# The last pair of heads turned through DRAM, and free places for the first turned tiles

## The chip, the cores and the metric

The kernel runs on one core of one Trainium2 chip. The metric is the time of one execution on the device in microseconds (us); the time before is the median of three runs. The engines are PE (matrix products), DVE (vector), ACT (scalar activations), POOL (GpSimd) and SP, whose queue issues most of the DMAs. DRAM is the chip's memory outside the cores; SBUF and PSUM are on the core, and PE writes its results to PSUM, eight banks of 128 x 512 float32.

## What is computed

One layer of a streaming encoder, in float32: four token mixers on `h = RMSNorm(x)`, gated and merged, then cross-attention, then a gated MLP. SEQ is 512, D_MODEL 1024. What matters here is mixer B, the forgetting attention, with 8 heads of 64 channels:

```python
s = jnp.einsum('bqhd,bkhd->bhqk', q_blk, k, preferred_element_type=jnp.float32) * scale
s = s + c_blk[..., None] - c_k[:, :, None, :]
mask = t_pos[None, :] <= tq_blk[:, None]
p = jax.nn.softmax(jnp.where(mask, s, -jnp.inf), axis=-1)
return jnp.einsum('bhqk,bkhd->bqhd', p.astype(v.dtype), v)
...
br = jnp.stack([ya, yf, yc, ys], axis=2)
proj = jnp.einsum('bsnc,ncd->bsnd', br, w_branch[l])
gates = jax.nn.sigmoid(h @ w_gate[l] + b_gate[l]).reshape(B, S, N_BRANCH, D)
mixed = jnp.sum(gates * proj, axis=2) @ w_out[l]
```

The mask is causal, so a query tile of 128 rows needs 128, 256, 384 or 512 keys. `yf` is the result of mixer B; its product with `w_branch` is the last of the four branches that the kernel adds up.

## The kernel before

Every float32 product is made as three products of a high and a low part (`mm3`: high by high, high by low, low by high), so a block of 128 output channels, 512 tokens and 1024 input channels takes 24 matrix products of 128 x 128 by 512. `channel_major` makes such a block. Weights come by SP in loads of 512 KB into two buffers `wr`; ACT and DVE split them into a high and a low tile (L198, L199).

The foreground is a list of such blocks, `mixer_jobs`. For the forgetting attention it has the projections of values and forget gates (`vf_jobs`), then for each of four pairs of heads two blocks for queries and keys (`kv_blocks`, L1199), with blocks of the gates and of branch A between them: `ga` yields 12 blocks in the order gate, gate, branch, and they stand 3 behind pair one's projections, 3 behind pair two's and 6 behind pair three's. Then the rest of the pairs is drained, and `last_branch_jobs` begins: gate, gate, branch and so on again, where a branch block (4 k-steps, one for each pair of heads) reads the result `y["f"]` of the pairs.

The pairs run in the background. `f_task` is a generator; at each `yield` it gives a cost and a time in which it isn't to be called again. `Background` (L47) calls the first two tasks of its queue at every tick (twice in a block), as long as it has credit, which grows by 0.7 of the foreground's estimated time and is at most 4. This sets the order of the program. A scheduler then orders each engine's instructions by that order and by its own estimate of when they are ready, and sets the waits.

A pair has four query tiles of 128 rows, one in each of the steps 0 to 3:

- `scores` (L830): 2 products for each head into an `sc` bank; DVE adds the bias and takes the row's minimum of the negated scores (L1129) into a tile `e`; ACT exponentiates (L1135); the two heads are scaled by ACT (L1142) and DVE (L1140). `e4()` has three buffers.
- The tile must then be turned so that keys lie on the partitions. Pairs 0 to 2 (`far`) do it through DRAM: `turn_ready` turns squares of 32 x 32 on DVE (`turn_squares`, L854) into another `e` tile, `put` (L859) stores that to DRAM, `get` (L866) loads it in another order into the low tile `ptl`, and `split_in_place` makes the high part on ACT (L872) and the low part on DVE (L873). The loads stand in steps 3 (query tiles 0, 1) and 5 (tiles 2, 3), the splits in steps 4 and 6, the products with the values in steps 5 and 7.
- Pair 3, the last, turns on PE: `to_keys_major` (L836) transposes each 128 x 128 piece with the identity (L247) into a `tr` bank, and ACT and DVE split it out of PSUM (L161, L162). It has six steps, with the values in steps 3 and 5. At its step 2 `share_now("mm")` takes the bank `tr0` from the gates' blocks.
- `pt_tiles` has two buffers each of `pth` and `ptl`; a pair of heads takes both for tiles 0 and 1, and both again for tiles 2 and 3. So a pair waits at step 3 (pair three: step 2) until the pair before it has made its last values (`f_steps[p - 1] < 8`).
- The two heads' results are in two `av` banks, the only ones; ACT and DVE add the high and the low part (L1153, L1154) and split the sum into `y["f"][0][:, p]` and `y["f"][1][:, p]`. These two tiles, of four places of 512 columns each, are made when the first pair ends.

The queries and keys of a pair lie in a tile with the tag `qk`, of which there are two.

Of the kernel before, what the change touches and what calls it, by code (L numbers as in the profile page):

```python
# [18 lines left out]
F32R = mybir.dt.float32r  # L19
# [6 lines left out]
P = 128  # L26
S = 512
# [56 lines left out]
def hybrid_layer(ctx: ExitStack, tc: tile.TileContext, a: dict, out: bass.AP):  # L84
# [21 lines left out]
    def share_now(*among):  # L106
        vars(turn_of).update(n=1, among=among)
# [102 lines left out]
    steps_of = []  # L210
# [110 lines left out]
    m1p = m1.__enter__()  # L321
# [211 lines left out]
    half = {}  # L533
# [74 lines left out]
    def y8(dtype=F32R):  # L608
        return m2p.tile([P, 4, S], dtype, tag="y8", name="y8", bufs=2)
# [5 lines left out]
    y = {}  # L615
# [249 lines left out]
    def get(d, n, pt, local):  # L865
        SP.dma_start(part_of(pt[1], n, local).bitcast(F32), d.rearrange("(a j) (b x) -> (j b) a x", j=32, b=4))  # L866

    def split_in_place(n, pt, local):
        hi, lo = (part_of(x, n, local) for x in pt)
        raw = lo.bitcast(F32)  # L870
        with tc.issue_after(evacuations[0]):
            A.copy(hi, raw)  # L872
        V.tensor_tensor(lo, raw, hi.bitcast(F32), ALU.subtract)  # L873
# [21 lines left out]
    def pt_tiles():  # L895
        return tuple(m1p.tile([P, 2, 4, 4, 32], F32R, tag=n, name=n, bufs=2) for n in ("pth", "ptl"))
# [160 lines left out]
    f_steps = {-1: 8}  # L1057

    def f_task(p, qk, v):
        f_steps[p] = 0  # L1060
        far = p < 3
        while f_steps[p - 1] < 4:
            yield 0.0, 0.5
        ck = []
        for j in range(2):
            t = m1p.tile([P, S], F32, tag="ck", name="ck", bufs=2)
            G.dma_start(t, crows[2 * p + j:2 * p + j + 1, :].rearrange("a s -> (a s)").partition_broadcast(P))
            ck.append(t)
        yield 0.0, 2.0 if p else 5.0
        es, pts, av, ready = {}, None, None, []  # L1070

        def turn_ready():
            while ready:
                qt, e, w = ready.pop()
                turned = e4()
                for j in range(2):
                    turn_squares(turned[:, j, :w], e[:, j, :w])
                es[qt] = put(turned, w)
        for step in range(8 if far else 6):
            if step in ((5, 7) if far else (3, 5)):  # L1080
                if av is None:
                    av = [bank("av"), bank("av")]
                with tc.issue_after(steps_of[0]) if far else ExitStack():
                    for j in range(2):
                        hl = v[0][:, :, 2 * p + j]
                        values(av[j], lambda kt: ((hl[:, kt], 0), (hl[:, kt], 1)), pts[j],
                               step // 2 - (2 if far else 1))
            while step == (3 if far else 2) and f_steps[p - 1] < 8:
                yield 0.0, 0.5
            f_steps[p] = step + 1  # L1090
            cost = 0.0
            if step == 4:
                turn_ready()
            if far:
                for qt in SPLITS.get(step, ()):
                    for j in range(2):
                        split_in_place(qt + 1, pts[j], qt % 2)
                    cost += 0.1 + 0.3 * qt
                for qt in GETS.get(step, ()):
                    if qt % 2 == 0:  # L1100
                        pts = [pt_tiles() for _ in range(2)]
                    d = es.pop(qt)
                    for j in range(2):
                        get(d[:, j], qt + 1, pts[j], qt % 2)
            else:
                if step == 2:
                    share_now("mm")
                for qt in {2: (0, 1), 3: (2,), 4: (3,)}.get(step, ()):
                    if qt % 2 == 0:
                        pts = [pt_tiles() for _ in range(2)]  # L1110
                    e = es.pop(qt)
                    for j in range(2):
                        to_keys_major(e[:, j], qt + 1, pts[j], qt % 2)
                    cost += 0.4 + 0.3 * qt
            if step < 4:
                qt, w = step, (step + 1) * P
                e = es[qt] = e4()
                st = m1p.tile([P, 8], F32, tag="st8", name="st8", bufs=4)
                for j in range(2):
                    head = 2 * p + j  # L1120
                    bias = m1p.tile([P, S], F32, tag="fbias", name="fbias", bufs=2)

                    G.tensor_scalar(bias[:, :w], ck[j][:, :w], -1.0, cq[:, qt, head:head + 1],  # L1123
                                    ALU.mult, ALU.add)
                    G.affine_select(out=bias[:, w - P:w], in_=bias[:, w - P:w], pattern=[[-1, P]],
                                    compare_op=ALU.is_ge, fill=BIG, base=0, channel_multiplier=1)
                    ps = bank("sc")
                    scores(ps, qk, j, qt * P, w)
                    low = V.tensor_tensor_reduce(e[:, j, :w], ps[:, :w], bias[:, :w], scale=-HD ** -0.5,  # L1129
                                                 scalar=3.0e38, op0=ALU.add, op1=ALU.min,  # L1130
                                                 accum_out=st[:, j:j + 1])
                with tc.issue_after(low.ins):
                    turn_ready()
                for j in range(2):
                    A.activation(e[:, j, :w], e[:, j, :w], AF.Exp, bias=st[:, j:j + 1],  # L1135
                                 scale=-1.0, accum_out=st[:, 4 + j:5 + j])
                V.reciprocal(st[:, 6:8], st[:, 4:6])
                for j in range(2):
                    if j:
                        V.tensor_scalar(e[:, j, :w], e[:, j, :w], st[:, 6 + j:7 + j], None, ALU.mult)  # L1140
                    else:
                        A.activation(e[:, j, :w], e[:, j, :w], AF.Copy, scale=st[:, 6 + j:7 + j])  # L1142
                cost += 0.6 + 0.0038 * w
                if far:
                    ready.append((qt, e, w))
                    cost += 0.003 * w
            yield cost, 6.5 if far and step == 5 else 4.5
        if "f" not in y:
            y["f"] = (y8(), y8())

        e = e4()
        for j in range(2):
            A.copy(e[0:HD, j], av[j][HD:P])  # L1153
            V.tensor_tensor(e[j * HD:(j + 1) * HD, 0], av[j][0:HD], e[0:HD, j], ALU.add)  # L1154
        split(e[:, 0], y["f"][0][:, p], y["f"][1][:, p])
        yield 1.8, 0.0
# [45 lines left out]
    def mixer_jobs():  # L1202
# [32 lines left out]
        ga = gate_blocks(0, "a")  # L1235
        for p in range(1, 4):
            yield from kv_blocks(p)
            for _ in range((3, 3, 6)[p - 1]):
                yield next(ga)
        yield then(lambda: bg.drain("f"))  # L1240

# [656 lines left out]
```

## Time and profile before

| | us |
|---|---|
| median of 3 runs | 1048.19 |
| lowest, highest | 1047.79, 1048.29 |
| the profiled execution | 1047.26 |
| its span on the core | 1045.5 |

The profile is one execution, seen by the hardware profiler. It gives each engine's busy time and the groups of its instructions, the chain of work that ended last (followed back from the last instruction, at each step to what released it), and timelines. The start of the span is 0. PE's instructions overlap: a product of 512 columns is in the timeline with 0.39 us, and the next starts 0.23 us after it. L247 is the line of the transposition, L241 that of every product; the tiles' names (`ps_tr`, `ps_mm`, `ps_av`, `ps_sc` for the banks, `y8b` for branch A's and `y` for the forgetting attention's results) tell them apart. In the columns of a timeline stand the start, the duration, the engine, the line, what is written and read, and in brackets the idle time before and what ended it.

### The profile page before, as it was taken

What the parts mean: (1) busy time and instruction counts of PE and PEld (TensorE: products, weight loads), DVE (VectorE), ACT (ScalarE), POOL (GpSimd) and SP (SyncE); (2) the same over time, 40 slices, a digit from 0 to 9 for tenths busy, and PEclk for the clock granted to TensorE, in tenths of its full rate; (3) what the DMA queues carried; (4) which work ended last, traced back from release to release, by engine and by line L of the source; (5) the groups of instructions that cost most, each with busy time, mean ns of one, the idle gap of its engine ahead of it and who ended that gap; (6) DMA issues with size and microseconds to landing.
All of it is one profiled execution on the core that took longest, in us unless ns stands there. A gap on an engine that the chain in (4) does not pass through costs nothing.

```text
span 1045.5 us, 14417 instructions
## 1 busy us (share of the span) xinstructions
PE 1035.8 (99%) x5235; PEld 880.7 (84%) x5235; DVE 809.6 (77%) x1241; ACT 510.6 (49%) x838; POOL 143.3 (14%) x239
## 2 busy tenths in 40 slices
PE   9999999999999999999999999999999999999997
PEld 8888888888888988888888899998888888888886
DVE  7999998677787367878577898777767777667786
ACT  5322222376565365666444566555343333445662
POOL 4001000100010123342101031121112111111001
PEclk9999999999999999999999999999999999999999
DMA  8954333334433246666338744135676676626662
GB/s 271 311 156 100 101 101 101 91 91 121 142 104 109 62 122 178 184 165 158 120 124 287 237 134 127 62 108 184 193 240 229 214 227 217 220 82 183 216 214 82
DMA packets 187453, 166.48 MB, mean 159 GB/s; under 512 B 20415, under 2 KB 159148, under 8 KB 187381
## 3 DMA queue, kind: packets, MB, share of 16 engines
q1 hardware_dynamic: 178339, 133.80, 43.1%
q10 hardware_dynamic: 6482, 23.21, 6.1%
q0 software_dynamic: 2560, 8.54, 2.7%
q8 instruction: 41, 0.67, 0.3%
q14 instruction: 31, 0.25, 0.1%
HBM read 140.74 MB, written 24.79 MB: 158 GB/s over the span
## 4 chain that ended last, share of the span: by engine, by line
PE 99%; DMA 0%; DVE 0%; issue 0%; POOL 0%; POOLq 0%; DVEq 0%; SPq 0%; ACT 0%; ACTq 0%
PE ps_mm L241 47%; PE ps_av L241 30%; PE ps_tr L241 11%; PE ps_sc L241 7%; PE ps_tr L247 2%; PE ps_mm L459 1%; PE ps_av L459 1%; DMA xs<-in_x 0%; PE ps_tr L443 0%; DVE o L1788 0%; PE ps_av L443 0%; DVE nt L438 0%; DVE ge L1183 0%; DVE nt L412 0%; POOL st_m L285 0%
## 5 line engine op out<-in xcount | busy, mean ns | idle before, releaser
L198 ACT CAST wh<-wr 128x1024 fp32r<-128x1024 f32 (+1 forms) x140 | 146.5, 1047 | 233.5 <-PE ps_mm L241 121.2
L199 DVE TENSOR_TENSOR wl<-wr,wh 128x1024 fp32r<-128x1024 f32 (+1 forms) x140 | 174.8, 1249 | 86.2 <-ACT wh L198 85.4
L241 PE MATMUL ps_mm<-hth,wh 128*128 128x512 f32 (+1 forms) x536 | 198.9, 378 | 0.0
L241 PE MATMUL ps_mm<-htl,wh 128*128 128x512 f32 (+1 forms) x536 | 198.3, 377 | 0.0
L241 PE MATMUL ps_mm<-hth,wl 128*128 128x512 f32 (+1 forms) x536 | 198.3, 377 | 0.0
L241 PE MATMUL ps_av<-hth,wh 128*128 128x512 f32 (+1 forms) x328 | 122.5, 374 | 0.0
L241 PE MATMUL ps_av<-htl,wh 128*128 128x512 f32 (+1 forms) x328 | 122.5, 373 | 0.0
L241 PE MATMUL ps_av<-hth,wl 128*128 128x512 f32 (+1 forms) x328 | 122.3, 373 | 0.0
L241 PEld LDWEIGHTS ps_mm<-hth,wl 128*128 128x128 f32 x536 | 99.0, 188 | 18.3
L241 PEld LDWEIGHTS ps_mm<-hth,wh 128*128 128x128 f32 x536 | 99.0, 188 | 17.9 <-ACT hth L161 0.3
L241 PEld LDWEIGHTS ps_mm<-htl,wh 128*128 128x128 f32 x536 | 98.9, 188 | 17.9
L694 DVE SCALAR_TENSOR_TENSOR y<-y,par,y 128x508 f32<-128x508 f32 (+29 forms) x120 | 82.5, 725 | 0.1
L241 PEld LDWEIGHTS ps_av<-hth,wh 128*128 128x128 f32 x328 | 61.6, 188 | 11.1 <-DVE e L1154 0.3
L241 PEld LDWEIGHTS ps_av<-htl,wh 128*128 128x128 f32 x328 | 61.6, 188 | 10.9
L241 PEld LDWEIGHTS ps_av<-hth,wl 128*128 128x128 f32 x328 | 61.6, 188 | 10.9
L1689 DVE TENSOR_TENSOR wl<-dw,wh 128x1024 fp32r<-128x1024 f32 x32 | 40.2, 1260 | 15.0 <-ACT wh L1688 14.7
L1688 ACT CAST wh<-dw 128x1024 fp32r<-128x1024 f32 x32 | 33.4, 1051 | 22.2 <-PE ps_mm L241 7.4
L1636 ACT ACTIVATE th<-c 128x512 f32<-128x512 f32 x22 | 13.9, 632 | 48.8 <-DVE c L621 48.8
L1123 POOL TENSOR_SCALAR fbias<-ck,cq 128x128 f32<-128x128 f32 (+3 forms) x32 | 23.4, 739 | 73.0 <-DVE st L1129 66.6
L621 DVE SCALAR_TENSOR_TENSOR c<-ps_mm,par,c 128x510 f32<-128x510 f32 (+1 forms) x44 | 32.7, 744 | 0.7
L241 PE MATMUL ps_tr<-hth,wh 128*128 128x512 f32 x80 | 31.8, 398 | 0.0
L241 PE MATMUL ps_tr<-htl,wh 128*128 128x512 f32 x80 | 31.6, 395 | 0.0
(503 smaller groups left out, 2227.9 us busy)
## 6 DMA issues: line engine op xcount, KB each, us to landing
wr<-in_w_up SPq DMA_DIRECT2D x44, 512.0 KB
wr<-in_w_in SPq DMA_DIRECT2D x38, 512.0 KB
wr<-in_w_gate SPq DMA_DIRECT2D x32, 512.0 KB
wp<-in_w_down ACTq DMA_DIRECT2D x22, 512.0 KB
sums<-wp ACTq DMA_DIRECT2D x22, 512.0 KB
dw<-sums SPq DMA_DIRECT2D x44, 256.0 KB
wr<-in_w_branch SPq DMA_DIRECT2D x16, 512.0 KB
wide<-in_w_out SPq DMA_DIRECT2D x12, 512.0 KB
```

What stands on the lines that cost most here:

```text
L198: last_weights[:] = [order(A.copy(hi, raw[:, :n])).ins, low.tensor_tensor(lo, raw[:, :n], hi.bitcast(F32), ALU.subtract).ins]
L199: low.tensor_tensor(lo, raw[:, :n], hi.bitcast(F32), ALU.subtract).ins]
L241: steps_of[:] = [PE.matmul(ps, lhs, rhs, start=start, stop=stop).ins]
L247: turns.append(PE.transpose(ps, x, ident[:n, :n]).ins)
L459: keep(PE.matmul(banks[c][:, :S // 2], w[p == 1][:, k, c * P:(c + 1) * P], ht[p == 2][:, i * 4 + k, :S // 2], start=(i, p, k) == (0, 0, 0) ...
L621: ins = V.scalar_tensor_tensor(dst[:, s:], src[:, :S - s], w(k), dst[:, s:], ALU.mult, ALU.add)
L694: ins = V.scalar_tensor_tensor(dst[:, s:], src[:, :S - s], pc("conv_dw", k * 4 + j), dst[:, s:], ALU.mult, ALU.add)
L1123: G.tensor_scalar(bias[:, :w], ck[j][:, :w], -1.0, cq[:, qt, head:head + 1], ALU.mult, ALU.add)
L1636: A.activation(th, c[:, 0], AF.Silu)
L1688: A.copy(hi, x)
L1689: V.tensor_tensor(lo, x, hi.bitcast(F32), ALU.subtract)
```

## The change

All four pairs go through DRAM in eight steps; `far` and pair three's way over PE are gone, with the change of the banks' share at its step 2. A pair's query tiles 0 and 1 no longer use `pth` and `ptl`: `first_tiles` puts them, for pairs 0 to 2, into places 2 and 3 of the two tiles of `y["f"]` (place 2 for the first head, 3 for the second), which only pairs two and three write in the end, and for pair three into a tile `half` with the tag `qk`. `y["f"]` is therefore made when a pair begins. The wait on the pair before is now for its step 6 at step 3 and for its step 8 at step 5. The gates' blocks stand 2, 3 and 7 behind the projections of pairs one, two and three. The planner's cost of a step of scores is the one that pairs 0 to 2 had.

```diff
     def f_task(p, qk, v):
         f_steps[p] = 0
-        far = p < 3
...
         yield 0.0, 2.0 if p else 5.0
+        if "f" not in y:
+            y["f"] = (y8(), y8())
         es, pts, av, ready = {}, None, None, []
+
+        def first_tiles():
+
+            free = m1p.tile([P, 6, S], F32R, tag="qk", name="half", bufs=2) if p == 3 else None
+            return [tuple((free[:, 2 * j + i] if p == 3 else y["f"][i][:, 2 + j]).rearrange(
+                "p (l a t i) -> p l a t i", l=2, a=4, t=2) for i in range(2)) for j in range(2)]
...
-        for step in range(8 if far else 6):
-            if step in ((5, 7) if far else (3, 5)):
+        for step in range(8):
+            if step in (5, 7):
                 if av is None:
                     av = [bank("av"), bank("av")]
-                with tc.issue_after(steps_of[0]) if far else ExitStack():
+                with tc.issue_after(steps_of[0]):
...
-                               step // 2 - (2 if far else 1))
-            while step == (3 if far else 2) and f_steps[p - 1] < 8:
+                               step // 2 - 2)
+            while f_steps[p - 1] < {3: 6, 5: 8}.get(step, 0):
                 yield 0.0, 0.5
...
-            if far:
-                for qt in SPLITS.get(step, ()):
...
-            else:
-                if step == 2:
-                    share_now("mm")
-                for qt in {2: (0, 1), 3: (2,), 4: (3,)}.get(step, ()):
-                    if qt % 2 == 0:
-                        pts = [pt_tiles() for _ in range(2)]
-                    e = es.pop(qt)
-                    for j in range(2):
-                        to_keys_major(e[:, j], qt + 1, pts[j], qt % 2)
-                    cost += 0.4 + 0.3 * qt
+            for qt in SPLITS.get(step, ()):
+                for j in range(2):
+                    split_in_place(qt + 1, pts[j], qt % 2)
+                cost += 0.1 + 0.3 * qt
+            for qt in GETS.get(step, ()):
+                if qt % 2 == 0:
+                    pts = [pt_tiles() for _ in range(2)] if qt else first_tiles()
+                d = es.pop(qt)
+                for j in range(2):
+                    get(d[:, j], qt + 1, pts[j], qt % 2)
...
-                cost += 0.6 + 0.0038 * w
-                if far:
-                    ready.append((qt, e, w))
-                    cost += 0.003 * w
-            yield cost, 6.5 if far and step == 5 else 4.5
-        if "f" not in y:
-            y["f"] = (y8(), y8())
-
+                ready.append((qt, e, w))
+                cost += 0.6 + 0.0068 * w
+            yield cost, 6.5 if step == 5 else 4.5
...
-            for _ in range((3, 3, 6)[p - 1]):
+            for _ in range((2, 3, 7)[p - 1]):
                 yield next(ga)
```

9 lines of the change are left out of this document (removed).

## The prediction

> **What bounds the kernel now.** I read the page first: which engine is full, at which clock, and whether the chain that ended last leaves that engine anywhere.
>
> ```profile
> PE 1035.8 (99%) x5235; PEld 880.7 (84%) x5235; DVE 809.6 (77%) x1241; ACT 510.6 (49%) x838; POOL 143.3 (14%) x239
> PEclk9999999999999999999999999999999999999999
> PE 99%; DMA 0%; DVE 0%; issue 0%; POOL 0%; POOLq 0%; DVEq 0%; SPq 0%; ACT 0%; ACTq 0%
> ```
>
> PE is the bound, at full clock, without holes. Work on DVE, ACT or SP is free as long as PE never waits for it. So I followed the chain of waits through the stretch that the change touches (the last two pairs of the forgetting attention, 440 to 540 us):
>
> ```profile
> 486.22 5.46 PE ps_mm L241 x24
> 491.67 0.22 PE ps_tr L247 x2
> ...
> 506.60 0.35 PE ps_tr L247 x3
> ...
> 514.63 0.44 PE ps_tr L247 x4
> ...
> 527.18 0.02 issue
> 527.21 0.70 DVE ge L1183
> 527.90 0.04 issue
> ```
>
> The first row is a block of 24 products, 0.23 us each. L247 are pair three's transpositions, seven pieces in all: 2, 2, 2, 3, 3, 4 and 4 of them, 20 together, at 0.11 to 0.12 us each. The last three rows are the only hole, 0.76 us, in which PE waits for DVE to empty an `mm` bank. That PE reaches it shows how tight the end is. The timeline of PE shows why:
>
> ```profile
> 466.88 1.08 PE L241 MATMUL ps_sc<-qk 128*128 128x512 f32 x4
> ...
> 495.53 0.27 PE L241 MATMUL ps_av<-ptl,v 128*128 128x128 f32 x1
> 495.64 1.15 PE L241 MATMUL ps_sc<-qk 128*128 128x512 f32 x4
> ...
> 518.47 0.27 PE L241 MATMUL ps_av<-ptl,v 128*128 128x128 f32 x1
> 518.58 0.69 PE L241 MATMUL ps_av<-y,wh 128*128 128x512 f32 x2
> ...
> 525.65 0.39 PE L241 MATMUL ps_mm<-y,wh 128*128 128x512 f32 x1
> ```
>
> Pair two's fourth scores run at 466.88 and its last value product at 495.53; pair three's at 495.64 and 518.47. PE goes on at 518.58 with a product in an `av` bank, and such a bank is free only when pair three's result has left it (`av` has two buffers, a pair holds both). By 518.58 PE has done everything that needs no result of pair three: the gates, the first three of four k-steps of the last branch's first block. I call the end of pair three's last value product V; V = 518.58 before, and what follows V is the same in both kernels. So the change is worth the shift of V.
>
> **What it removes.** 20 transpositions on PE: 0.22 + 0.22 + 0.22 + 0.35 + 0.35 + 0.44 + 0.44 = 2.24 us, all in the chain. If pair three's data are there in time, V comes at 518.58 - 2.24 = 516.34, and no earlier, for PE is full up to there. The hole at 527.18 comes from an order in which the last k-step of the first block (525.65) stands behind a whole gate; it can close where pair three is early against that order (-0.76) or stay (0). I count 0, as the banks behind it (`mm`, `av`) are shared as before. The dropped switch to `mm` alone gives the gates one bank more until the last branch sets its own share; I count 0, since the chain shows no wait for a bank before 527.18, and the bound for a gain is that same hole.
>
> **What it adds off PE.** Per query tile and head one 32x32 turn on DVE, one in-place split in place of an evacuation of PSUM, and 4 stores and 8 loads on SP's queue.
>
> ```profile
> 469.35 1.63 DVE L854 STREAM_TRANSPOSE e<-e 128x384 f32<-128x384 f32 x2 [0.40 <-DMA turned<-e]
> ...
> 478.15 1.10 DVE L854 STREAM_TRANSPOSE e<-e 128x512 f32<-128x512 f32 x1
> ...
> 480.88 1.07 DVE L854 STREAM_TRANSPOSE e<-e 128x512 f32<-128x512 f32 x1
> ...
> 500.24 0.69 DVE L162 TENSOR_TENSOR y<-e,y 128x512 fp32r<-128x512 f32 x1 [0.69 <-ACT y L161]
> 501.10 0.69 DVE L1129 CUSTOM_DVE_ANT_0 e<-ps_sc,fbias 128x512 f32<-128x512 f32 x1 [0.17 <-PE ps_mm L241]
> ```
>
> The two wide turns cost 2.17 us on DVE, the two of 384 columns 1.63, the smaller ones less than that: under 6.0 us. They lie beside PE where DVE has room:
>
> ```profile
> 500.00:505.00 5.00, 5.00 (x26) 4.09 (x24) 3.29 (x9) 3.29 (x8) 0.00 (x0) 1.00 0.73 217
> 505.00:510.00 5.00, 5.00 (x31) 4.34 (x30) 3.39 (x5) 3.64 (x7) 0.00 (x0) 1.00 0.37 106
> 510.00:515.00 5.00, 5.00 (x28) 4.14 (x27) 0.91 (x2) 0.59 (x1) 0.00 (x0) 1.00 0.37 105
> 515.00:520.00 5.00, 5.00 (x31) 4.41 (x30) 2.60 (x3) 2.74 (x4) 0.00 (x0) 1.00 0.00 0
> 525.00:530.00 5.00, 4.90 (x22) 3.74 (x21) 2.79 (x4) 3.04 (x4) 0.99 (x2) 1.00 0.00 0
> ```
>
> The columns are PE, PEld, DVE, ACT and POOL busy, the clock, the DMA share and GB/s. From 500 to 520 DVE is busy 10.19 of 20 us, so 9.8 us are free. Cost 0; were DVE full, the two last turns would move V by up to their 2.17 us. On SP the transfers stand in one line with the loads of weights:
>
> ```profile
> 481.98 0.37 SPq L859 DMA_DIRECT2D turned<-e  x1
> ...
> 486.27 0.91 SPq L866 DMA_DIRECT2D ptl<-turned  x2
> ...
> 506.05 4.10 SPq L182 DMA_DIRECT2D wr<-in_w_gate  x2
> 520.01 0.37 SPq L182 DMA_DIRECT2D wr<-in_w_branch  x1
> ```
>
> A load of a tile that waits at the head of SP's queue for its store holds the weights behind it by 4.29 us at most (481.98 to 486.27); between 510.15 and 520.01 SP issues nothing, so I count 0.
>
> **What moves.** Each pair's turned tiles 0 and 1 get places of their own, so step 3 waits for the former pair's sixth step instead of its eighth, and a block of gates goes behind pair three's projections. I followed the planner's clock by the source (24 products of 512 columns count 5.16, a step waits 4.5, credit grows by 0.7). Before, pair three's first two scores stand behind the 18th and 19th block since pair 0, as the trace has them; after, in the middle of these, half a block (12 products) earlier. The third stand just ahead of the drain instead of in it, the fourth still in it, behind pair two's last values. So the end of the chain starts where it did, near 495.64, and only what is ahead of it gains. The pairs before cost nothing new: same blocks, same steps, PE full.
>
> **The one term that can spoil it** is the way through DRAM in the last pair. Its price, from pair two's rows and one store of branch A:
>
> ```profile
> 462.60 1.18 DVE L854 STREAM_TRANSPOSE e<-e 128x256 f32<-128x256 f32 x2
> ...
> 494.65 0.55 DVE L1129 CUSTOM_DVE_ANT_0 e<-ps_sc,fbias 128x384 f32<-128x384 f32 x1
> ```
> ```profile
> 490.79 0.62 ACT L872 CAST pth<-ptl 128x512 fp32r<-128x512 f32 x1 [1.71 <-DMA ptl<-turned]
> ...
> 503.00 0.73 ACT L1135 ACTIVATE e<-e,st 128x512 f32<-128x512 f32 x1
> ...
> 505.49 0.74 ACT L1142 ACTIVATE e<-e,st 128x512 f32<-128x512 f32 x1
> ```
> ```profile
> 248.56 0.33 SPq L859 DMA_DIRECT2D turned<-e  x1
> 251.12 0.36 SPq L866 DMA_DIRECT2D ptl<-turned  x1
> ```
>
> From fourth scores to last store: pair two took 481.98 - 466.88 = 15.1 us, with DVE busy for other things and one wait for a store (0.40). The bare work is 1.15 scores + 1.38 (two L1129) + 1.46 (two exponentials) + 0.74 scaling + 2.17 turns = 6.9. From last store to V: pair two took 13.7 (481.98 to 495.64). Of this 8.81 are the round trip (481.98 to 490.79); with two casts behind it (1.24), a subtraction as long as L1129 (0.69) and the second head's eight products (put at 0.83), 11.6. So V lies between 495.64 + 6.9 + 11.6 = 514.1 and 495.64 + 15.1 + 13.7 = 524.4. Against the 516.34 that PE allows, the term is 0 to +8.1.
>
> Between the ends decide the three `e` tiles. Before, the fourth scores' softmax starts on DVE at 501.10, 5.46 us after its scores, since its tile comes free only with PE's transpositions of the second score tile. After, that tile is free once DVE has turned it: third scores taken in at 494.65 + 0.55, turn 1.18, so 496.4. But a turn needs a further `e` tile, held until its store has landed. The turn of the second tile holds one until its store lands: 4.29 us by pair two's last store, 2.56 by a smaller one of branch A (248.56 to 251.12); it has half the columns of the first, so I take 3: 499.4. Then the third turn (1.63): 501.0. The tile that this frees goes to pair two's result, which stands earlier in the program, and the fourth turn waits for that or for the third store, 3.6 us by the same two rows: 504.6. With 2.17 the last store is at 506.8 and V = 506.8 + 11.6 = 518.4; less the half block's effect on the tiles ahead, which I put at 0.8 of its 2.7 us (12 x 0.23), as only the first two scores move: 517.6. PE then waits 517.6 - 516.34 = **1.3 us** ahead of pair three's last values. I choose that over pair two's 15.1 since from 505 on DVE and ACT are nearly idle, which they weren't for pair two, and over 0 since each turn hangs on a store.
>
> Sum: -2.24 + 1.3 + 0 = about -1.0 us against the profiled execution of 1047.26 us (span 1045.5, 1.76 outside it), so 1046.3 there; the median of the runs, 1048.19, lies 0.93 above it, so **1047.2**.
>
> [...]
>
> **Rivals.**
> - *The whole gain.* Stores that land as fast as branch A's (2.56) and a third turn that finds its tile at once put the last store at or before 504.7; V = 516.34, no wait: -2.24, 1045.9; where the hole at 527.18 closes as well, -3.0, 1045.2. For: the softmax that starts 4.7 us earlier, the idle DVE. Against: three tiles for two pairs.
> - *Slower: the `e` ring holds the last turn.* If pair two's result takes the tile of the second turn ahead of the third turn, it keeps it from 495.64 to 500.24 + 0.69 in the rows of before, 5.3 us, and the third turn, its store and the fourth come that much later in place of the 3 that I count for a store. From a last store at 509.1 on (V = 520.7) the kernel is slower by over 0.2%; with pair two's own 15.1 and 11.6, V = 522.3, +3.8, 1052.0. For: pair two's turns also waited for a store. Against: the tile can go to either, and the third turn stands first in the program.
> - *The free places bring no overlap*: the planner's credit, not the wait, sets when the third and fifth step come. Then the half block's 0.8 is missing and V = 518.4, -0.2: 1048.0, inside the forecast's case.
> - *The wait lowers PE's clock.* If PE stands still for several us ahead of V and runs its next 24 products at half clock, these cost 24 x 0.23 = 5.5 us more: 1052.0 + 5.5 = 1057.5. Against: the hole of 0.76 left the clock at 1.00 (last row of the windows). [...]
>
> **How the numbers follow.** A measurement of this kernel can tell 0.2% (2.1 us) from no change. Forecast's case, with the one without overlap (V from 516.6 to 520.6, -2.0 to +2.0 us, 1046.2 to 1050.2): 0.35, all within 0.2%. The whole gain 0.34: faster. The ring 0.28 and the clock 0.03: slower, 0.31. Cases of both signs hold most of the chance, so the range is wide: from 1045.0 (both gains and 0.2) to 1051.4, which leaves out of the slower cases what is above +3.2, about half of them (0.16), and 0.03 below.
>
> **What would show it.** Right: no transposition on L247 between 480 and 530, the fourth scores near 495, the last store (L859 of 512 columns) near 506, an idle time of PE of 1 to 2 us ahead of pair three's last values, released by DVE L873 or ACT L872. Whole gain: no such idle time. Wrong: a fourth turn that starts after 507, or waits for anything but a store or pair two's result. It would all be wrong if PE's order around the earlier pairs opened holes, since I count none there, or if V were not what the last branch waits for.

## The result, and the profile after

| | before | after |
|---|---|---|
| median of 7 runs each, us | 1047.79 | 1051.73 |
| lowest, highest | 1047.08, 1049.58 | 1049.90, 1053.08 |
| the profiled execution | 1047.26 | 1051.54 |
| its span | 1045.5 | 1049.7 |

The ratio is 1.0036, with a 95% interval of 1.0026 to 1.0046: about 3.8 us slower, where the forecast was 1047.2 and the range ended at 1051.4.

First the same three lines of the page as before, now of the kernel after.

```profile
PE 1037.1 (99%) x5215; PEld 881.4 (84%) x5215; DVE 812.9 (77%) x1249; ACT 511.0 (49%) x838; POOL 140.4 (13%) x239
PEclk9999999999999999999899999999999999999999
PE 97%; DMA 1%; DVE 1%; ACT 0%; issue 0%; POOL 0%; POOLq 0%; SPq 0%; DVEq 0%; ACTq 0%
```

PE has the 20 instructions less (5235 before), yet the chain that ended last spends 2% more of the span off PE, and one slice of the clock reads 8. Where it leaves PE is in the chain of waits after, 495 to 535 us, a stretch in which the chain of before left PE only at 527.18:

```profile
496.29 0.37 PE ps_sc L241 x2
...
503.09 3.14 DMA ptl<-turned
...
509.00 9.34 DMA wr<-in_w_gate
...
521.37 7.37 PE ps_av L241 x24
```

For 25 us, from pair three's fourth scores to the last branch's next products in an `av` bank, something else sets the pace, and the longest piece is a DMA of 9.34 us, a load of weights for a gate. PE's waits in the stretch from 505 to 535 us (total, times, longest), of which the kernel before has none that this view lists:

```profile
PE ps_av L241 <- ACT pth L872: 2.6, 2, 2.4
PE ps_av L241 <- DVE e L1145: 0.6, 1, 0.6
```

L872 is the cast of a turned tile, L1145 the addition that was L1154 before. The timeline of PE after shows the places:

```profile
514.67 0.39 PE L241 MATMUL ps_av<-pth,v 128*128 128x256 f32 x1 [0.28 <-ACT pth L872]
...
517.64 0.39 PE L241 MATMUL ps_av<-pth,v 128*128 128x256 f32 x1 [2.36 <-ACT pth L872]
517.87 0.28 PE L241 MATMUL ps_av<-ptl,v 128*128 128x256 f32 x1
...
520.36 0.41 PE L241 MATMUL ps_av<-ptl,v 128*128 128x128 f32 x1
521.37 1.22 PE L241 MATMUL ps_av<-y,wh 128*128 128x512 f32 x2 [0.59 <-DVE e L1145]
...
525.17 0.40 PE L241 MATMUL ps_av<-hth,wh 128*128 128x512 f32 x1
```

V, the end of pair three's last value product, is at 520.36 + 0.41 = 520.77. The forecast was 517.6, and PE alone would have allowed 516.34. The nine products that follow at 521.37 are the first three k-steps of the last branch's second block. They read the results of pairs zero to two only (pair three's is written by ACT at 522.15 and DVE at 522.80); what they wait for is the `av` bank of pair three's first head, which the addition L1145 empties. They take 525.17 - 521.37 = 3.80 us; before, they took 520.75 - 518.58 = 2.17, as this row of the timeline of before shows beside the one at 518.58:

```profile
520.75 0.50 PE L241 MATMUL ps_av<-hth,wh 128*128 128x512 f32 x1
```

So PE waits 0.28 + 2.36 + 0.59 = 3.23 us, and behind the second wait it runs at half speed. The windows after say so (columns as before: PE, PEld, DVE, ACT, POOL, clock, DMA share, GB/s):

```profile
505.00:510.00 5.00, 5.00 (x28) 4.22 (x27) 3.91 (x6) 2.56 (x4) 1.11 (x2) 1.00 0.83 242
510.00:515.00 5.00, 4.72 (x22) 3.60 (x20) 0.35 (x1) 0.62 (x1) 0.00 (x0) 1.00 0.83 252
515.00:520.00 5.00, 2.64 (x14) 2.36 (x13) 1.54 (x3) 2.18 (x3) 0.00 (x0) 0.81 0.45 153
520.00:525.00 5.00, 4.41 (x14) 3.49 (x13) 2.69 (x4) 1.27 (x3) 0.00 (x0) 0.51 0.32 105
```

They also say what the casts waited for. From 505 to 515 the DMA engines are busy 0.83 of the time, where before it was 0.37. The timeline of SP's queue after, the last store and the last loads:

```profile
504.73 0.36 SPq L859 DMA_DIRECT2D turned<-e  x1
506.18 0.37 SPq L182 DMA_DIRECT2D wr<-in_w_gate  x1
507.61 0.91 SPq L866 DMA_DIRECT2D ptl<-turned  x2
509.00 0.37 SPq L182 DMA_DIRECT2D wr<-in_w_gate  x1
```

The casts that take up these two loads, in the timeline of ACT after:

```profile
514.00 0.62 ACT L872 CAST pth<-ptl 128x512 fp32r<-128x512 f32 x1 [5.70 <-DMA ptl<-turned]
516.97 0.62 ACT L872 CAST pth<-ptl 128x512 fp32r<-128x512 f32 x1 [2.35 <-DMA ptl<-turned]
```

ACT stood idle for both, so the first load landed 514.00 - 507.61 = 6.4 us after the issue of the two and the second 9.4. The load of weights behind them took the 9.34 us of the chain (509.00 to 518.34), and the 0.59 us hang on it: its split stands on ACT (518.42) and DVE (519.50) ahead of the addition. The last store itself left early, at 504.73. What else was in flight stands in the timeline of POOL, first after, then before:

```profile
508.25 0.57 POOL L1257 DMA_DIRECT2D g_mem<-in_norm_mem  x1 [12.12 <-PE ps_av L241]
508.99 0.54 POOL L1291 DMA_DIRECT2D m_t<-in_mem  x1 [0.17 <-issue]
```
```profile
498.25 0.57 POOL L1266 DMA_DIRECT2D g_mem<-in_norm_mem  x1
498.99 0.54 POOL L1300 DMA_DIRECT2D m_t<-in_mem  x1 [0.17 <-issue]
```

These are the first two loads of the next stage, the cross-attention's memory: its gain, spread over the partitions, and a tile of 128 rows, 512 KB each. They belong to none of the lines that the change touches. Before, they ran at 498, and nothing of pair three went through DRAM. After, they run at 508, half a microsecond behind pair three's last loads, which are 256 KB each. What held them is in the view of the tile `half` after (who reads it, and who waited for it, in us):

```profile
L241 PE MATMUL ps_av<-half,v x8: 225/278/285, 506.0 to 507.7; 128*128 128x256 f32 x4, 128*128 128x128 f32 x4
...
  POOL g_mem L1257: 12.1, 1
```

`half`, the tile that the change puts into a `qk` place for pair three's first turned tiles, is read until pair three's first value products (the last starts at 507.7), and the loads of the next stage wait until it is done with. Tiles of the pairs' memory end there, and the next stage's tiles take their place.

### The profile page after: what moved, and what is told of

Its sections match the earlier page's. It is cut to its first block, busy times and chain, and to the rows that moved or that the text cites. A ratio compares the mean times of both kernels' runs of the same rounds, so it can differ in the third digit from the quotient of the medians.

```text
span 1049.7 us, 14408 instructions
## 1 busy us (share of the span) xinstructions
PE 1037.1 (99%) x5215; PEld 881.4 (84%) x5215; DVE 812.9 (77%) x1249; ACT 511.0 (49%) x838; POOL 140.4 (13%) x239
## 4 chain that ended last, share of the span: by engine, by line
PE 97%; DMA 1%; DVE 1%; ACT 0%; issue 0%; POOL 0%; POOLq 0%; SPq 0%; DVEq 0%; ACTq 0%
PE ps_mm L241 45%; PE ps_av L241 30%; PE ps_tr L241 11%; PE ps_sc L241 7%; PE ps_tr L247 2%; DMA wr<-in_w_gate 1%; PE ps_mm L459 1%; PE ps_av L459 1%; PE ps_mm L400 0%; DMA ptl<-turned 0%; PE ps_sc L405 0%; DVE wl L199 0%; DMA turned<-e 0%; ACT wh L198 0%; DVE e L854 0%
## 5 line engine op out<-in xcount | busy, mean ns | idle before, releaser
L198 ACT CAST wh<-wr 128x1024 fp32r<-128x1024 f32 (+1 forms) x140 | 146.6, 1048 | 239.7 <-PE ps_mm L241 131.1
L241 PE MATMUL ps_mm<-hth,wh 128*128 128x512 f32 (+1 forms) x528 | 195.4, 377 | 0.0
L241 PE MATMUL ps_mm<-htl,wh 128*128 128x512 f32 (+1 forms) x528 | 195.2, 377 | 0.0
L241 PE MATMUL ps_mm<-hth,wl 128*128 128x512 f32 (+1 forms) x528 | 195.0, 377 | 0.0
L241 PE MATMUL ps_tr<-hth,wh 128*128 128x512 f32 x88 | 34.8, 395 | 0.0
L241 PE MATMUL ps_tr<-htl,wh 128*128 128x512 f32 x88 | 34.7, 394 | 0.0
L241 PE MATMUL ps_tr<-hth,wl 128*128 128x512 f32 x88 | 34.7, 394 | 0.0
L854 DVE STREAM_TRANSPOSE e<-e 128x128 f32<-128x128 f32 (+3 forms) x44 | 31.4, 741 | 2.7 <-DMA turned<-e 2.5
```

Source lines behind the costliest of these rows:

```text
L198: last_weights[:] = [order(A.copy(hi, raw[:, :n])).ins, low.tensor_tensor(lo, raw[:, :n], hi.bitcast(F32), ALU.subtract).ins]
L241: steps_of[:] = [PE.matmul(ps, lhs, rhs, start=start, stop=stop).ins]
L854: V.transpose(dst, src.rearrange("p (t j b) -> p b t j", b=4, j=32))
```

## The experiments

They ran in four groups, each beside the kernel before on one chip. The medians of before were 1047.85 us (19 runs) in group A, 1047.30 (27) in B, 1047.20 (15) in C and 1047.30 (21) in D; A and D ran on the same chip, B and C on two others. In the kernels that hold a split, line numbers are shifted by 7 (L879 is L872, L1152 is L1145).

| kernel | group | median (lowest to highest, runs) | ratio to before |
|---|---|---|---|
| POOL's loads of the memory held | A | 1046.53 (1045.42 to 1047.27, 10) | 0.9987 [0.9978, 0.9996] |
| the same, again | D | 1045.90 (1045.44 to 1047.18, 11) | 0.9988 [0.9979, 0.9996] |
| after, blocks 3, 3, 6 | A | 1054.33 (1053.85 to 1054.69, 4) | 1.0059 [1.0044, 1.0074] |
| the same with the loads held | B | 1047.57 (1046.47 to 1049.10, 10) | 1.0002 [0.9993, 1.0012] |
| before, pair three through DRAM | A | 1055.01 (1053.99 to 1056.18, 4) | 1.0063 [1.0046, 1.0079] |
| the same with the loads held | C | 1051.49 (1051.31 to 1053.49, 4) | 1.0047 [1.0031, 1.0062] |
| before, blocks 2, 3, 7 | A | 1047.28 (1047.01 to 1047.72, 10) | 0.9992 [0.9983, 1.0002] |
| before, the loads held | B | 1047.52 (1047.03 to 1048.60, 10) | 1.0004 [0.9995, 1.0013] |
| after, 18 products in the wait | B | 1051.18 (1049.82 to 1052.41, 6) | 1.0038 [1.0026, 1.0050] |
| loads held, 2nd split held | B | 1047.52 (1046.67 to 1049.35, 10) | 1.0007 [0.9998, 1.0017] |
| loads held, 3rd split held | D | 1048.23 (1047.27 to 1049.61, 11) | 1.0012 [1.0003, 1.0021] |
| loads held, 4th split held | C | 1046.02 (1045.52 to 1048.19, 11) | 0.9989 [0.9981, 0.9998] |

### The kernel after, with POOL's loads of the memory held back

```diff
+        ns.late = G.tensor_copy(small["fe"][:, :1], y["f"][0][:, 3, :1].bitcast(F32)).ins
-        G.dma_start(ns.gain, a["norm_mem"][0].partition_broadcast(P))
+        with tc.issue_after(ns.late):
+            G.dma_start(ns.gain, a["norm_mem"][0].partition_broadcast(P))
...
-            G.dma_start(m_t, mem_d[t * P:(t + 1) * P, :])
+            with tc.issue_after(ns.late):
+                G.dma_start(m_t, mem_d[t * P:(t + 1) * P, :])
```

A copy of one column of pair three's result stands ahead of the two loads, so that they come once the pairs are done.

> The changed kernel, but POOL's loads of the memory's gain and tokens (L1257, L1291, together 1 MB) start only when pair three's result is in y. Theory A (they crowd out pair three's last two loads, which landed 6.4 and 9.4 us after their issue): these land at most 4.5 us after their issue, PE's idle time ahead of the last values falls below 0.5 us, the clock stays at 1.00, and the kernel takes 1045.3 to 1046.5 us, faster than before. Rival B (the way through DRAM itself and SP's own loads of weights are too slow at this place): landing still over 6 us, 1049.5 us or more.

It came out at 0.9987 of before: 5 us below the kernel after, and a little below the kernel before as well. POOL, ACT and PE in its timelines, and the load of weights in its chain:

```profile
519.97 0.58 POOL L1259 DMA_DIRECT2D g_mem<-in_norm_mem  x1
```
```profile
511.44 0.62 ACT L872 CAST pth<-ptl 128x512 fp32r<-128x512 f32 x1 [3.37 <-DMA ptl<-turned]
513.14 0.62 ACT L872 CAST pth<-ptl 128x512 fp32r<-128x512 f32 x1 [1.08 <-DMA ptl<-turned]
514.84 1.05 ACT L198 CAST wh<-wr 128x1024 fp32r<-128x1024 f32 x1 [1.07 <-DMA wr<-in_w_gate]
```
```profile
517.79 0.73 PE L241 MATMUL ps_av<-y,wh 128*128 128x512 f32 x2 [1.49 <-DVE e L1145]
```
```profile
508.77 5.99 DMA wr<-in_w_gate
```

The loads, issued at 507.46, land 4.0 and 5.7 us later in place of 6.4 and 9.4 (I had expected 4.5 at most), and the weights' takes 5.99 us in place of 9.34. PE no longer waits for a cast: V is at 517.79 - 1.49 = 516.30, the limit that the sum gave (516.34). The clock stays at 1.00. The one wait left is 1.49 us for the additions. They stand on ACT and DVE behind a split of weights (L198 at 514.84), which itself waited for its load; before, the first head's copy (517.16) stood ahead of that split (517.67), and its bank was free when PE came to it.

How the times compare is best read from PE's first product on `mix`, the merged branches (before, after, here):

```profile
566.17 0.39 PE L241 MATMUL ps_sc<-wh,mix 128*128 128x512 f32 x1
```
```profile
570.06 0.39 PE L241 MATMUL ps_sc<-wh,mix 128*128 128x512 f32 x1
```
```profile
564.84 0.39 PE L241 MATMUL ps_sc<-wh,mix 128*128 128x512 f32 x1
```

The kernel after stands 5.2 us behind this one there, as its median does: 521.37 - 517.79 = 3.6 ahead of the nine products and 3.80 - 2.17 = 1.6 in them. Against before, this kernel is 518.58 - 517.79 = 0.79 ahead at the nine products (2.24 less 1.49, but for 0.04) and 1.33 at `mix`; the ratio makes 1.4. In its profiled execution about 0.8 of this is lost again between 1020 and 1025 us, around a wait of 0.52 for L1683, and the spans differ by only 0.3 (1045.5 to 1045.2); the repeat has no such wait.

The repeat on the same chip, in a later group, said the same:

> The kernel with POOL's loads of the memory held, once more, beside the one above on the same chip. If the first result stands: 1045.5 to 1047.0, ratio to the kernel before 0.998 to 0.9995, loads landed within 4 to 6 us, no wait for the casts, one wait of 1.4 to 1.9 us for the additions.

0.9988; loads landed 3.8 and 5.4 us after their issue, PE waited 1.11 us for the additions, a little less than expected, and the span was 1044.1, 1.4 below that of before. So the change with these loads held beats both kernels, the one before by little more than 0.1%.

### The control: the loads held in the kernel before

The same edit in the kernel before.

> Control: the kernel before with POOL's two loads of the memory held in the same way. Theory A: these loads disturb nothing there (they ran at 498 us, between pair two's loads and no others), so within 0.8 us of before. Rival D (holding them is a gain of its own, whatever the pairs do): 1.3 us faster, as the first experiment was.

1.0004, as expected: the holding gains nothing by itself. In the changed kernel it is worth what it takes out of the way of pair three's loads and of the weights behind them.

### The blocks 3, 3, 6 in the kernel after

```diff
-            for _ in range((2, 3, 7)[p - 1]):
+            for _ in range((3, 3, 6)[p - 1]):
```

> The changed kernel with the gates' blocks at 3, 3 and 6 as before. Theory A: the traffic at the end is the same, so within 1.5 us of the changed kernel (1050.2 to 1053.2). Rival (the split 2, 3, 7 moves pair three into a bad place): at most 1048.5.

1.0059, and 1054.33 is above the 1050.2 to 1053.2 that my theory gave. The last loads are issued 2.5 us later than after, at 510.10, and the two casts stand at

```profile
518.31 0.62 ACT L872 CAST pth<-ptl 128x512 fp32r<-128x512 f32 x1 [8.15 <-DMA ptl<-turned]
519.11 0.62 ACT L872 CAST pth<-ptl 128x512 fp32r<-128x512 f32 x1 [0.18 <-DMA ptl<-turned]
```

so 8.2 us after their issue for the first. I had left out that POOL's loads move with them (509.66 and 510.41, as `half` is free later) and meet them again. PE waits 3.38 us in one piece (515.61 to 518.99), and the clock stays at half for longer, 10.2 us where it was 6.8 in the kernel after:

```profile
520.00:525.00 5.00, 4.51 (x18) 4.13 (x19) 2.96 (x4) 2.60 (x4) 0.00 (x0) 0.50 0.12 28
```

With the loads held as well:

> The second experiment (split 3, 3, 6) with the memory's loads held. Theory A (the traffic and the idle time that it makes are most of what the split 3, 3, 6 loses too): pair three's last loads land within 5 us and 1047 to 1049 us. Rival (the split itself puts the last store 2.3 us later and costs that whatever the traffic): 1051 or more.

1.0002. The loads landed within 3.2 us and 4.0 us (issued 509.96, casts 513.16 and 514.00). So nearly all of the 1.0059 is traffic and what follows from it. The half block moved by the change is worth some 1.5 us (1.0002 against 0.9987, on two chips, each to within 0.001), where the prediction gave it 0.8.

### The half block alone, in the kernel before

> The kernel before with the gates' blocks at 2, 3 and 7 alone. Theory A: no more than 1 us from before (1046.8 to 1048.8). Rival (the split is the harm): 1050 or more.

0.9992, as expected, and the view lists no wait of PE from 500 to 535 us: no effect that can be told from none.

### Pair three through DRAM, but in the old places

```diff
-        far = p < 3
+        far = True
```

> The kernel before with all four pairs through DRAM and nothing else: no free places, the old wait for the eighth step, split 3, 3, 6. Without the tile half in a qk place the memory's loads can go near 498 us as before, so theory A expects pair three's last loads undisturbed (4.5 us), but all of pair three's loads stand behind pair two's last values: 1047 to 1051. Rival C (the missing overlap is what costs, the free places are needed): 1053 or more.

1.0063: the rival's number, not the theory's. POOL's loads are no part of it in the way they are after: without `half` they stand where they stood in the kernel before (timeline of POOL):

```profile
498.37 0.71 POOL L1266 DMA_DIRECT2D g_mem<-in_norm_mem  x1 [0.48 <-issue]
```

That is also the second sign that `half` is what keeps them to 508. Here they run beside the loads of pair three's tile 0. And pair three's four loads for tiles 2 and 3 are late because `pth` and `ptl` must serve its tiles 0 and 1 first: they are issued from 511.81 on, and the casts follow from 517.19 to 521.40. With the loads held:

> The kernel before with pair three through DRAM (old places, blocks 3, 3, 6; ratio 1.0063 without more) and with POOL's loads of the memory held until the last pair's result is written. In that kernel POOL's loads ran at 498 to 500, not beside the last loads (issued 511.81 and 514.35). Theory: traffic was not what made it slow, the missing places were (step three waits for pair two's last values, so the turned tiles come late): the holding gains less than 2 us, the first cast of the last loads still comes after 515.5, and the time is 1052.5 to 1055.5. Rival: the last loads are slow there too for traffic of POOL's: they land within 4.5 us, the time is 1047 to 1050.5, and the free places are worth next to nothing once the traffic is gone.

1.0047, between the two theories: the holding gained 3.5 us (1055.01 to 1051.49, on two chips), as the second cast of tile 0 came at 501.94 in place of 504.73 and all that follows with it, and the first of the late casts came at 513.72, 5.4 us after the issue at 508.36, earlier than my theory had it. What remains to 0.9987 is 0.6%, about 6 us. Of this the free places, with the earlier step three, bring 4.7 (1.0047 to 1.0002, the changed kernel with blocks 3, 3, 6 and the loads held) and the half block the other 1.5. So both parts of the change work, once POOL's loads are out of the way.

### The clock: PE kept busy in the wait

```diff
+                if p == 3 and step == 7:
+                    ps_d = bank("tr")
+                    for _ in range(18):
+                        PE.matmul(ps_d[:, :256].rearrange("p (a i) -> p a i", i=32), v[0][:, 0, 2 * p],
+                                  pts[0][0][:, :, :, 0].rearrange("p l a i -> p (l a) i"), start=True, stop=True)
```

18 products that nobody reads, between the two loads' casts, in the kernel after.

> The changed kernel with 18 products of 256 columns that nobody reads (each 0.12 us) on PE between the two heads' last loads, reading the first head's part. They fill the 2.4 us of idle time and take nothing from it otherwise. Theory: the clock fell to 0.5 for some 7 us because PE stood idle, which cost about 2.7 us (16 value products and 9 products of 512 columns at twice their time); with PE busy it stays at 1.00 and the kernel takes 1048.0 to 1049.5. Rival (the lower clock is not from the idle time): 1051 or more, clock still below 1 from 515 to 525.

In the profiled execution, which took 1049.82, it did what it should:

```profile
514.47 2.40 PE L1093 MATMUL ps_tr<-pth,v 128*128 128x256 f32 x18
...
521.13 0.73 PE L241 MATMUL ps_av<-y,wh 128*128 128x512 f32 x2 [1.25 <-DVE e L1150]
```
```profile
520.00:525.00 5.00, 3.87 (x17) 3.21 (x18) 3.19 (x4) 2.52 (x5) 0.21 (x2) 1.00 0.32 99
```

The clock stays at 1.00 and the nine products run 0.23 us apart. The last value product ends at 519.59 instead of 520.77, but the nine products start at 521.13, only 0.24 earlier than after, as the addition still stands behind the weights' split on ACT (518.71). But the median of six is 1051.18, above what I expected, and no difference from the kernel after (1051.73) is shown; the other five runs had a mean clock of 0.995 to 0.997 where this one has 0.998. So the price of the clock is shown for one execution, about 1.7 us against after's profiled one, and one run of the kernel after, without the products, is as fast (1049.90 at a mean clock of 0.999). Why the clock fell in the other five, which have no trace, stays open.

### What is left: the split of weights ahead of the additions

Three kernels, each with the loads held and one of the splits of weights ordered behind pair three's last additions.

```diff
+        with ExitStack() as stack:
+            if len(behind) == 3:
+                for ins in behind[:2]:
+                    stack.enter_context(tc.issue_after(ins))
+                behind.clear()
+            elif behind:
+                behind.append(None)
-        last_weights[:] = [order(A.copy(hi, raw[:, :n])).ins,
-                           low.tensor_tensor(lo, raw[:, :n], hi.bitcast(F32), ALU.subtract).ins]
+            last_weights[:] = [order(A.copy(hi, raw[:, :n])).ins,
+                               low.tensor_tensor(lo, raw[:, :n], hi.bitcast(F32), ALU.subtract).ins]
...
+        if p == 3:
+            behind[:] = [c, s]
```

The count is 3 for the second split, 4 for the third, 5 for the fourth; `c` and `s` are the two last additions.

> The first experiment (memory's loads held), and the split of one gate block's weights (L198 on ACT, L199 on DVE) ordered behind pair three's last additions. Theory: the 1.49 us that PE still waits there for DVE's L1145 stand behind L199 in DVE's order, so they fall to under 0.6 and the kernel gains about 1 us: 1045.0 to 1046.0. Rival (the copy out of the av bank is late for another reason): no gain, 1046.5.

> The same as the run with the second split held, but the weights' split held behind pair three's last additions is the fourth after the drain (the first split is that of the first gate of the last branch, the fourth the first of gate m4). Theory: with the loads of the memory held, the 1.49 us in which PE waits for the additions come from a weights' split that stands ahead of them on ACT and DVE, and this is the split that does; the wait falls to about 0.5 us, no hole opens at 527 to 528, and the median is 1.0 us below that of the run with the loads held alone (1046.53): 1045.0 to 1046.2, ratio about 0.998. Rival: the held split is again not the one in front, or its products are then late themselves: a wait of 1 us or more at 517 to 518 or at 527 to 528, and 1046.3 or more.

> The same with the third weights' split after the drain held behind pair three's last additions. Holding the fourth left the split in front of the additions where it was, holding the second moved one that ran at 502 to 506. Theory: the third is the one at 514.8 to 517.1, so PE's wait for the additions falls from 1.5 to 1.8 us to about 0.5, no further hole opens, and the median is 0.8 to 1.3 us below that of the kernel with the loads held alone, which runs beside it: about 1045.2. Rival: its products come right behind the first ones of the last k-step and wait for it in turn (a wait of 1 us or more between 519 and 528), and the median is within 0.5 us of the kernel beside it or above it.

The second: the wait for the additions fell to 0.49, but the time did not (1.0007, where neither theory nor rival had it), and a new one stands on PE behind it:

```profile
516.66 0.74 PE L248 MATMUL ps_av<-y,wh 128*128 128x512 f32 x2 [0.49 <-DVE e L1152]
527.77 0.72 PE L248 MATMUL ps_mm<-y,wh 128*128 128x512 f32 x2 [1.98 <-DVE ge L1183]
```

The third: the same, 0.61 and 1.61, as the rival had it, and 2.3 us more than the kernel with the loads held beside it (1048.23, 1045.90). The reason is in the timeline of SP's queue with the third held:

```profile
507.59 0.91 SPq L873 DMA_DIRECT2D ptl<-turned  x2
519.30 0.37 SPq L182 DMA_DIRECT2D wr<-in_w_gate  x1
```

A split also frees the buffer `wr` that its raw weights lie in. Held, it keeps the next weights from being loaded at 508.8; they start at 519.30, are split only at 524.84, and the multiplication by the gate (L1183), which empties PE's bank, stands on DVE behind that split. The fourth: the time of the loads held alone, 0.9989, within what I expected, but not for my reason, since the split in front stayed and the profiled execution still waits 1.76 us for the additions. I found no version that takes this wait away without another.

By the way these kernels give the price of a load beside the last two.

| in flight beside the last two loads | landed after their issue, us |
|---|---|
| POOL's two, two of weights (after; with the 18 products) | 6.4 and 9.4; 5.9 and 9.3 |
| the same (blocks 3, 3, 6) | 8.2 and 9.0 |
| two of weights (loads held; again; fourth split held) | 4.0 and 5.7; 3.8 and 5.4; 4.0 and 6.0 |
| the same (loads held, blocks 3, 3, 6) | 3.2 and 4.0 |
| one of weights ahead (third split held) | 3.8 and 4.6 |
| one of weights behind (second split held) | 2.8 and 3.7 |

POOL's two loads separate them without exception: 5.9 us or more and 9.0 or more with them, at most 4.0 and 6.0 without. Among the kernels without them the number of loads alone doesn't set the order (3.2 and 4.0 stand with two); when each was issued differs too.

## Why the prediction was wrong, step by step

- **The 20 transpositions, -2.24 us on PE:** right. With the loads held, V is at 516.30, against 516.34 in the sum; by the starts of the last value product, 518.47 and 516.02, it is 2.45.
- **The free places, the `e` ring and the last store:** the mechanism held, and the term was too high by a little. The last store left at 504.73, forecast at 506.8 - 0.8 = 506.0. The rival of the `e` ring gave 1052.0, which is close to what was measured, but it is not what happened: it needed a last store from 509.1 on. The agreement of the numbers is chance. The whole gain had asked for a last store at or before 504.7. That came true within 0.03 us, and its V of 516.34 still came only with POOL's loads held.
- **The step that failed:** "between 510.15 and 520.01 SP issues nothing, so I count 0", together with the 11.6 us from the last store to V. I costed the transfers as a line on SP's queue and took the round trip as a fixed 8.81 us. I did not look at POOL's queue at 498 to 499 in the profile of before, where the two loads of the next stage stand, nor at what they wait for. The new tile `half` moves them by 10 us, into the one window in which the way through DRAM is bare. From last store to V it took 520.77 - 504.73 = 16.0 us; with the loads held, 516.30 - 504.57 = 11.7, and there PE, not the loads, set V. So the term of +1.3 came out as 520.77 - 516.34 = 4.4, of which 1.0 is half clock.
- **A second step that failed:** "what follows V is the same in both kernels". Behind V come 521.37 - 520.77 = 0.60 us for the additions, which stand behind a late load of weights, and 3.80 - 2.17 = 1.63 for the nine products at half clock. With -2.24 + 4.43 + 0.60 + 1.63 the first product of the next gate is 4.42 later than before, and the profiled span in the end 4.2, where the sum had -1.0. Even with POOL's loads held, 1.49 of the 2.24 go to the additions.
- **The round trip, taken as a fixed 8.81 us:** it is 9.3 us after (504.73 to the cast at 514.00), and 5.6 with the second split held (504.43 to 510.01), where POOL's loads are held and SP's weights come behind the two loads. The DMA engines are busy 0.83 over ten microseconds after, with loads of SP and of POOL in flight, and SP's land 2.4 and 3.7 us later than with POOL's held. That traffic on another queue is what spoke against this change, and I did not bring it in.
- **The clock:** the rival with a chance of 0.03 came true as a part. It fell to half after a wait of 2.36 us, not of several. The last 15 value products took 2.49 us (517.87 to 520.36) where 1.48 is their time with the loads held, and the nine products 1.63 more: 1.01 + 1.63 = 2.6 us of PE's time, where I had 5.5 for a stay of 24 products. Most of the 1.01 cost nothing more, since the additions were late anyway: with the 18 products V came 1.18 us earlier and the nine products only 0.24. My ground against it, the hole at 527.18, says nothing of such a wait, as PE hardly stood still there.
- **The hole at 527.18, counted 0:** it closed, but I had misread its size. The 0.76 us are the time for which the chain runs over DVE; PE itself had other products to run meanwhile, and lost 0.49 - 0.23 = 0.26 us between the two starts below, in the timeline of before. In the kernel after, the shift from before falls from 4.42 at the first product of the next gate to 570.06 - 566.17 = 3.89 at `mix`.

```profile
527.46 0.39 PE L241 MATMUL ps_av<-hth,wl 128*128 128x512 f32 x1
527.95 0.73 PE L241 MATMUL ps_mm<-y,wh 128*128 128x512 f32 x2
```

- **The turns on DVE, the bank's share, the earlier pairs, counted 0:** right as far as the trace goes. No wait of PE is listed from 440 to 500 us in the kernel after, and DVE is busy 0.35 of 5 us from 510 to 515.

## What to carry to other kernels

A tile put into a "free" place has a next owner: look up who takes that memory afterwards, and when, on every queue, also for work of the next stage that the change never names. A transfer that becomes the critical one has to be costed with all that is in flight beside it, on all queues (here the same two loads landed after 6.4 and 9.4 us, and after 4.0 and 5.7 with POOL's held), and an order that keeps a later stage's prefetch out of that window can be worth more than the change itself (5 us here, against 2.24 from the work removed), though in the kernel before the same order gained nothing. Where a wait is put ahead of the bounding engine, add what its clock may lose behind the wait (here a wait of 2.36 us was followed by 6.8 us at half clock).

## What the runs showed of the hardware

How short a wait can halve the clock was not expected, nor that a longer one may not. With the fourth split held, PE waited 1.76 us once, up to 518.09, and ran at half clock behind it; with the second split held it waited 1.98 us, up to 527.77, and did not. The first four rows are of the former, the other three of the latter:

```profile
516.00:518.00 2.00, 0.33 (x4) 0.18 (x2) 1.78 (x2) 1.25 (x3) 0.00 (x0) 1.00 0.00 0
518.00:520.00 2.00, 1.91 (x6) 1.53 (x7) 1.28 (x3) 0.62 (x1) 0.53 (x1) 0.76 0.71 217
520.00:522.00 2.00, 2.00 (x6) 1.56 (x5) 0.13 (x1) 0.00 (x0) 1.30 (x3) 0.50 0.34 92
522.00:524.00 2.00, 2.00 (x9) 1.62 (x9) 0.00 (x0) 0.00 (x0) 0.00 (x0) 0.89 0.95 266
```
```profile
526.00:528.00 2.00, 0.23 (x1) 0.23 (x2) 2.00 (x3) 1.66 (x2) 0.00 (x0) 1.00 0.00 0
528.00:530.00 2.00, 2.00 (x10) 1.61 (x10) 2.00 (x4) 0.99 (x3) 1.54 (x2) 1.00 0.85 262
530.00:532.00 2.00, 2.00 (x10) 1.65 (x9) 2.00 (x4) 1.47 (x2) 0.50 (x1) 1.00 0.17 48
```

How long the clock was at half is an estimate from the clocks of such windows, of 2 or of 5 us: 0.76, 0.50 and 0.89 above make 2 x (0.48 + 1.00 + 0.22) = 3.4 us. The table has it for the stretch from 505 to 535 us, with PE's longest wait there, or the waits that stood close together.

| kernel | PE waited, us | clock then |
|---|---|---|
| after, blocks 3, 3, 6 | 3.38 | half for 10.2 us |
| after | 2.36 | half for 6.8 |
| second split held | 1.98 | 1.00 |
| loads held, blocks 3, 3, 6 | 1.82 | half for 3.4 |
| fourth split held | 1.76 | half for 3.4 |
| third split held | 1.61 | 1.00 |
| loads held | 1.49 | 1.00 |
| after, 18 products | 1.25 | 1.00 |
| loads held, again | 1.11 | 1.00 |
| before, pair three through DRAM, up to 511.69 | 1.64 | 1.00 |
| the same, up to 524.87 | 1.61, 0.34 and 1.04 within 4.4 | half for 6.8 |
| before, pair three through DRAM, the loads held | 1.62, 0.34 and 1.03 within 4.4 | half for 3.4 |

So the length of one wait doesn't separate these traces: 1.76 and 1.82 us were followed by half clock and 1.98 was not, and a wait of 1.6 us was followed by it only where another of 1.0 came soon behind. What does separate them, and why the clock stayed down for 3.4 us in one and for 10.2 in another, they do not show.

The runs without a trace differ as well, though no wait is shown for them: with the second split held six of ten lie between 1046.67 and 1047.62 at a mean clock of 0.998 or 0.999 and four between 1048.96 and 1049.35 at 0.997, with the third five of eleven are at 0.997 and none of them below 1049.10, and the profiled execution with the fourth is at 1048.19 and 0.996 the longest of its eleven. The kernel after took 1049.90 at 0.999, 1050.47 to 1052.00 at 0.996, 1052.49 and 1053.08 at 0.993. By an estimate from the table, 3.4 us at half clock take 3.4 x 0.5 / 1046 = 0.0016 from the mean clock.
